# Splitting the weights of every sublayer by transfers of GpSimd's queue

## The chip, the cores and the metric

The kernel runs on one core of a Trainium2 chip. A core has five engines that run side by side, each through its own queue of instructions in order: TensorE (PE; the loading of its weights is shown as PEld), VectorE (DVE), ScalarE (ACT), GpSimd (POOL) and SyncE (SP), which here only issues transfers. Sixteen DMA engines move data between memory and the on-chip buffers. The metric is the device time of one execution in microseconds (us), lower is better.

## The reference, cut to what matters

Two blocks follow each other on x of 512 tokens x 1024 features, in float32. The first has two layers of three sublayers: a feed forward, a mixer (stick-breaking attention in layer 0, a gated linear recurrence in layer 1) and a second feed forward, each behind a norm and a modulation by shift, scale and gate that come from a vector c. The second block has two hybrid layers with three attentions and gates. All heavy work is products of activations with float32 weights:

```python
def swiglu(h, w_gu, w_down):
    g, u = jnp.split(h @ w_gu, 2, axis=-1)
    return (jax.nn.silu(g) * u) @ w_down
...
        h, g = sublayer_input(x, norm_g[layer, 0], mod[:, 0])
        x = x + MACARON_W * g * swiglu(h, ffn_w_gu[layer, 0], ffn_w_down[layer, 0])
```

## The kernel before

Activations are kept transposed, features on the 128 partitions and the 512 tokens along the row. TensorE takes a rounded format (float32r) at its full rate, so that each float32 operand is split in two rounded parts, high and low, and every product is made of three matmuls: high by high, high weight by low activation, low weight by high activation (`proj`, lines 571 to 585; `proj_tok`, 587 to 601, has the weights as the moving side).

All weights come from one array `ws` of blocks of 128 x 1024 that the host has put in the order of use. The order is a list of entries (`layout`, line 197): a weight entry ("w") holds eight slots of 128 x 128; an entry "mod" holds a block of the modulation matrix. There are 493 weight entries and 144 modulation blocks. The eight segments are named ffn00, sb, ffn01, ffn10, lru, ffn11, hy0 and hy1. In ffn00 56 and in ffn10 48 modulation blocks stand between the weights, in ffn01 24, and 16 at the very start.

`stream_dma` (line 451) issues the loads ahead on SP's queue, of 512 KB each, into a ring of four tiles `raw` (`RAW = 4`, line 319), shared by both kinds of entry. `stream_step` (line 476) takes the next entry. A modulation block is multiplied with c and summed by DVE (line 485). A weight entry is split in two chunks of 512 columns, each in three steps: ACT copies the chunk, rounding it, to `wh` (line 497; in one stretch of the recurrence, where `act_busy` is set at line 1319, DVE does it at line 495), and POOL or DVE subtracts the copy from the raw weights into `wl` (line 503). Which of the two is chosen by a credit (`pool_low`, lines 498 to 502): POOL in the mixers, in the hybrid layers and at the start of a sublayer, DVE in the rest of the feed forwards. `wh` and `wl` have five buffers each (`AHEAD + 1`). After the split of the second chunk the raw tile is free (line 513).

```python
    def ahead(self, c):
        while self.w_conv < c + 1 + self.look and self.e_conv < len(self.entries):
            self.stream_step()
```

`take` (line 558) hands TensorE's code the high and low part of the next slots and calls `ahead`, so that the split is written into the program four chunks ahead of the use. At the start of each sublayer of the first block the shift part of the modulation is not known in time; there the products are made without it and a correction is summed by DVE from the plain raw weights (`shifts`, line 518; `first_slots`, line 177, lists these slots).

The order of instructions on an engine comes from two sources. The mixers' steps are generators that `pump` starts when a count of TensorE's time (`vt`) has passed their `yield`; within `with self.tc.manual_schedule()` (in `begin`, line 870, and at the kernel's start) the written order holds, and elsewhere a scheduler orders each engine's queue by the priority of the written order and its own model of times. Waits between engines, and for a free buffer of a tile's ring, are put in by the framework.

Other work that the steps of the prediction touch: POOL's selection in the stick-breaking attention (line 1132), its squares of the residual (lines 635 and 639), its sums of gates (line 1816); DVE's split of rotated queries and keys (line 1375); ACT's square roots and gates in the recurrence (lines 1277 and 1284); SP's copies of queries and keys into stacked tiles (line 981) and the loads and stores of x (lines 833 and 1880).

Of the kernel before, what the change touches and what calls it, by code (L numbers as in the profile page):

```python
# [22 lines left out]
F32 = mybir.dt.float32  # L23
F32R = mybir.dt.float32r
I32 = mybir.dt.int32
AF = mybir.ActivationFunctionType
OP = mybir.AluOpType
# [149 lines left out]
def first_slots(segs):  # L177

    out = {}
    slot = 0  # L180
    for name, jobs, _ in segs:
        for job in jobs:
            for kt in rows_of(job):
                for j, (_, _, cols) in enumerate(job[1]):
                    if name in LATE and job[0] == "first":
                        out[slot] = (LATE[name], kt, j)
                    elif name == "ffn00" and job[0] in ("gu6", "gu7"):
                        out[slot] = ((0, 0), kt, int(job[0][2:]))
                    slot += len(cols) // 128
    return out  # L190


def rows_of(job):
    return range(job[2]) if isinstance(job[2], int) else job[2]
# [120 lines left out]
class Kern:  # L315
# [117 lines left out]
    def stream_init(self, entries):  # L433
        self.entries = entries
        self.e_dma = 0
        self.e_conv = 0
        self.raws = {}
        self.parts = {}
        self.slot = 0
        self.w_conv = 0  # L440
        self.n_w, self.kept = 0, []
        self.in_ring = 0
        self.full = set()
        self.wshift = {}
        self.inv = None
        self.look = self.AHEAD
        self.act_busy = False
        self.pool_low = 0.0
        self.pool_credit = 0.0

    def stream_dma(self):
        nc = self.nc
        while self.e_dma < len(self.entries):
            src = self.io["ws"][self.e_dma]
            e = self.entries[self.e_dma]
            if e[0] == "w" and self.n_w < self.KEEP:
                raw = [self.t("keep"), self.t("keep")]
                self.n_w += 1
                for j in range(2):
                    nc.sync.dma_start(raw[j], src[:, 512 * j:512 * j + 512])  # L460
            elif self.in_ring < self.RAW:
                raw = self.wpool.tile([128, 1024], F32, name=self.name("raw"), tag="raw", bufs=self.RAW)
                nc.sync.dma_start(raw, src)
                self.in_ring += 1
                if e[:2] == ("mod", (0, 0, 1)):
                    x = self.t("x")
                    nc.sync.dma_start(x, self.io["xT"][e[2]])
                    if e[2] == 4:
                        nc.sync.dma_start(self.ident, self.io["k_ident"])
                    self.x.append(x)  # L470
            else:
                break
            self.raws[self.e_dma] = raw
            self.e_dma += 1

    def stream_step(self):
        self.stream_dma()
        e = self.entries[self.e_conv]
        raw = self.raws[self.e_conv]
        nc = self.nc  # L480
        if e[0] == "mod":
            vec, m = e[1], e[2]
            if vec not in self.mods:
                self.mods[vec] = self.modp.tile([128, 8], F32, name=self.name("mod"), tag="mod", bufs=12)
            nc.vector.tensor_tensor_reduce(raw, raw, self.cact, 1.0, 0.0, OP.mult, OP.add, accum_out=self.mods[vec][:, m:m + 1])  # L485
            self.full.add((vec, m))
            if m == KD - 1 and vec != (0, 0, 1):
                self.mod_end(vec, 0, KD)
        else:
            j = self.w_conv % 2  # L490
            w = raw[j] if type(raw) is list else raw[:, 512 * j:512 * j + 512]
            h = self.wpool.tile([128, 512], F32R, name=self.name("wh"), tag="wh", bufs=self.AHEAD + 1)
            l = self.wpool.tile([128, 512], F32R, name=self.name("wl"), tag="wl", bufs=self.AHEAD + 1)
            if self.act_busy:
                nc.vector.tensor_copy(h, w)
            else:
                nc.scalar.copy(h, w)  # L497
            self.pool_credit += self.pool_low
            eng = nc.vector
            if self.pool_credit >= 1.0:  # L500
                self.pool_credit -= 1.0
                eng = nc.gpsimd
            eng.tensor_tensor(l, w, h.bitcast(F32), OP.subtract)  # L503
            self.parts[self.w_conv] = (h, l)
            if type(raw) is list:
                self.kept.append((4 * self.w_conv, w))
            else:
                self.shifts(w, 4 * self.w_conv)
            self.w_conv += 1
            if j == 0:  # L510
                return
        if type(raw) is not list:
            self.in_ring -= 1
        del self.raws[self.e_conv]
        self.e_conv += 1
        self.stream_dma()
# [41 lines left out]
    def take(self, n):  # L558
        c, o = divmod(self.slot, 4)
        self.ahead(c)  # L560
        self.parts.pop(c - 1, None)
        self.slot += n
        h, l = self.parts[c]
        return h[:, 128 * o:128 * (o + n)], l[:, 128 * o:128 * (o + n)]
# [1334 lines left out]
    def body(self):  # L1899
        nc = self.nc  # L1900
        segs = segments()
        self.stream_init(layout(segs))
        self.segs = {n: list(j) for n, j, _ in segs}
        self.late = first_slots(segs)
        self.mods = {}
        self.twice = False
        self.quick = False
        self.sq = {}
        self.gain, self.save, self.hnext, self.xd = None, False, [], []
        self.vecs = self.const.tile([128, NVEC], F32, name="vecs")  # L1910
        self.ident = self.const.tile([128, 128], F32, name="ident")
        self.ones = self.const.tile([128, 128], F32, name="ones")
        self.cact = self.const.tile([128, 1024], F32, name="cact")

        def shown(name):
            if self.upto == name:
                for m in range(KD):
                    nc.sync.dma_start(self.io["out"][m], self.x[m])
                return True

        for l in range(2):
            for i in range(2):
                self.jobs = self.segs[f"ffn{l}{i}"]
                if (l, i) == (1, 1):
                    self.twice = self.save = True
                    self.fgain = self.modp.tile([128, 8], F32, name="gain")
                    nc.vector.tensor_tensor(self.fgain, self.vec("final_norm_g"), self.vec("norm_g_2", 0, 8), OP.mult)
                self.ffn(l, i)
                if shown(f"ffn{l}{i}"):
                    return  # L1930
                if i:
                    continue
                if l == 0:
                    self.jobs = self.segs["sb"]
                    self.stick()
                else:
                    with self.tc.manual_schedule():
                        self.lru_consts()
                    self.jobs = self.segs["lru"]
                    self.lru()  # L1940
                if shown("sb" if l == 0 else "lru"):
                    return
        self.hybrid_consts()
        for l in range(2):
            self.jobs = self.segs[f"hy{l}"]
            self.hybrid(l)
            if shown(f"hy{l}"):
                return
        self.last_norm()
# [28 lines left out]
```

## Time and profile before

| | us |
|---|---|
| median of 3 runs | 3132.27 |
| lowest and highest | 3131.87, 3133.31 |
| the profiled execution, its own time | 3133.14 |
| its span, first to last instruction | 3131.3 |
| TensorE busy in the span | 3007.2 |
| DVE, ACT, POOL busy | 1921.7, 1321.7, 1072.8 |

The span is what the trace sees of an execution; 1.84 us lie around it. A row of a group gives the line, engine and operation, the tiles written and read, the shapes, the count, then busy time, the mean of one in ns, and the engine's idle time just before with what ended it. Instructions that only issue a transfer or wait are not counted as busy. "DMA share" is the mean busy share of the sixteen DMA engines.

### The profile page before, as it was taken

The numbers are of one execution on the slowest core, as the hardware profiler recorded it, in microseconds if no ns is written. First come the engines' busy times: TensorE is split into PE (matmuls) and PEld (weight loads), VectorE is DVE, ScalarE is ACT, GpSimd is POOL, SyncE is SP. The second block draws the span as 40 slices with busy tenths as digits, with TensorE's granted clock in tenths as the row PEclk, the third lists the DMA queues.
The fourth block names the chain that finished last, engine by engine and source line by source line (L and its number), as shares of the span: only waits on it lengthen the run. The fifth ranks groups of instructions, "written<-read, shape, count | busy, mean of one in ns | idle before, by whom it ended". The sixth has DMA issues, their size and how long they took to land. (4 is left out here: it accounts for less than half of the span.)

```text
span 3131.3 us, 39192 instructions
## 1 busy us (share of the span) xinstructions
PE 3007.2 (96%) x13752; PEld 2474.4 (79%) x13752; DVE 1921.7 (61%) x3455; ACT 1321.7 (42%) x2520; POOL 1072.8 (34%) x828
## 2 busy tenths in 40 slices
PE   7999999989999999999899999999999999999998
PEld 5788877778888888887788888888787778878776
DVE  7844467685445654569773334587766547877643
ACT  3332245543332333226543333355455434655552
POOL 4455744440001100025430002433334674333356
PEclk9999999999999999999999999999999999999999
DMA  6454545324343344542222223543441336324322
GB/s 243 163 195 172 209 120 142 102 68 147 130 140 128 135 162 149 181 175 74 88 88 101 94 105 111 136 135 105 120 132 62 108 124 177 103 88 128 102 78 91
DMA packets 132358, 400.03 MB, mean 128 GB/s; under 512 B 18496, under 2 KB 19008, under 8 KB 132160
## 3 DMA queue, kind: packets, MB, share of 16 engines
q1 hardware_dynamic: 132160, 397.51, 39.1%
q8 instruction: 109, 1.79, 0.2%
q14 instruction: 89, 0.73, 0.1%
HBM read 342.91 MB, written 6.30 MB: 112 GB/s over the span
## 5 line engine op out<-in xcount | busy, mean ns | idle before, releaser
L503 POOL TENSOR_TENSOR wl<-raw,wh 128x512 fp32r<-128x512 f32 x576 | 803.0, 1402 | 940.9 <-ACT wh L497 897.2
L497 ACT CAST wh<-raw 128x512 fp32r<-128x512 f32 x968 | 596.4, 620 | 1152.7 <-PE mm L417 993.0
L417 PE MATMUL mm<-hH,wh 128*128 128x512 f32 x1584 | 620.9, 392 | 12.4 <-ACT ge L1284 9.8
L417 PE MATMUL mm<-hL,wh 128*128 128x512 f32 x1584 | 620.3, 392 | 4.1 <-DVE hL L722 3.4
L417 PE MATMUL mm<-hH,wl 128*128 128x512 f32 x1584 | 619.4, 391 | 0.3 <-POOL wl L503 0.3
L503 DVE TENSOR_TENSOR wl<-raw,wh 128x512 fp32r<-128x512 f32 x394 | 290.0, 737 | 363.0 <-ACT wh L497 360.6
L417 PE MATMUL mm<-gH,wh 128*128 128x512 f32 x1016 | 409.7, 403 | 1.9 <-ACT wh L497 1.8
L417 PE MATMUL mm<-gH,wl 128*128 128x512 f32 x1016 | 401.9, 396 | 1.3 <-POOL wl L503 1.3
L417 PE MATMUL mm<-gL,wh 128*128 128x512 f32 x1016 | 401.6, 395 | 0.0
L417 PEld LDWEIGHTS mm<-hH,wh 128*128 128x128 f32 x1584 | 299.1, 189 | 76.0 <-ACT ge L1284 10.2
L417 PEld LDWEIGHTS mm<-hL,wh 128*128 128x128 f32 x1584 | 299.0, 189 | 68.5 <-DVE hL L722 5.5
L417 PEld LDWEIGHTS mm<-hH,wl 128*128 128x128 f32 x1584 | 298.9, 189 | 62.3 <-POOL wl L503 0.7
L485 DVE CUSTOM_DVE_ANT_0 raw<-raw,cact 128x1024 f32<-128x1024 f32 x144 | 209.2, 1456 | 177.4 <-DMA raw<-ws 167.0
L417 PE MATMUL mm<-aH,wh 128*128 128x512 f32 x704 | 273.9, 389 | 0.0
L417 PE MATMUL mm<-aH,wl 128*128 128x512 f32 x704 | 273.9, 389 | 0.0
L635 POOL TENSOR_TENSOR sq<-x 128x512 f32<-128x512 f32 x7 | 8.1, 1151 | 736.9 <-DVE x L970 710.0
L417 PEld LDWEIGHTS mm<-gH,wl 128*128 128x128 f32 x1016 | 192.4, 189 | 42.1 <-POOL wl L503 2.6
L417 PEld LDWEIGHTS mm<-gH,wh 128*128 128x128 f32 x1016 | 193.4, 190 | 36.2 <-ACT wh L497 2.3
L417 PEld LDWEIGHTS mm<-gL,wh 128*128 128x128 f32 x1016 | 193.3, 190 | 32.9
L1029 DVE TENSOR_TENSOR wide<-T,wide 128x128 fp32r<-128x128 f32 (+3 forms) x192 | 94.2, 511 | 102.5 <-ACT wide L1026 93.8
L417 PEld LDWEIGHTS mm<-aH,wh 128*128 128x128 f32 x704 | 132.1, 188 | 27.6
L417 PEld LDWEIGHTS mm<-aH,wl 128*128 128x128 f32 x704 | 132.1, 188 | 27.4
(302 smaller groups left out, 4825.0 us busy)
## 6 DMA issues: line engine op xcount, KB each, us to landing
raw<-ws SPq DMA_DIRECT2D x629, 512.0 KB, 3.3
ks<-rH SPq DMA_DIRECT2D x80, 128.0 KB, 3.1
kl<-rL SPq DMA_DIRECT2D x80, 128.0 KB, 2.4
qs<-rH SPq DMA_DIRECT2D x56, 128.0 KB, 3.9
qs<-rL SPq DMA_DIRECT2D x56, 128.0 KB, 3.9
keep<-ws SPq DMA_DIRECT2D x16, 256.0 KB, 5.7
ks<-qkH SPq DMA_DIRECT2D x32, 128.0 KB, 2.8
kl<-qkL SPq DMA_DIRECT2D x32, 128.0 KB, 2.4
```

What stands on the lines that cost most here:

```text
L417: self.nc.tensor.matmul(out, lhsT, rhs, start=start, stop=stop, skip_group_check=True)
L485: nc.vector.tensor_tensor_reduce(raw, raw, self.cact, 1.0, 0.0, OP.mult, OP.add, accum_out=self.mods[vec][:, m:m + 1])
L497: nc.scalar.copy(h, w)
L503: eng.tensor_tensor(l, w, h.bitcast(F32), OP.subtract)
L635: nc.gpsimd.tensor_tensor(q, self.x[m], self.x[m], OP.mult)
L1029: nc.vector.tensor_tensor(dst(pt[1], o, n, step), src(c, n, step), dst(pt[0], o, n, step).bitcast(F32), OP.subtract)
```

## The change

A weight entry without any slot that needs the plain weights (and not among the first eight) is loaded from POOL's queue into the raw tile with its type given as float32r, which rounds it: the tile is then the high part itself, and no `wh` is made. For each chunk ACT writes the negated high part to `wl`, and a second transfer from POOL's queue adds the plain weights from memory to it, which leaves the low part. The raw tile counts as used until TensorE's code has gone past its second chunk (`held`); the release is looked at in `take`. By the layout 464 of the 493 weight entries take this way: 58 in ffn00, 28 in sb, 62 in each of ffn01, ffn10 and ffn11, 28 in lru, 82 in each of hy0 and hy1.

```diff
--- before.py
+++ after.py
@@ -187,6 +187,25 @@
                     elif name == "ffn00" and job[0] in ("gu6", "gu7"):
                         out[slot] = ((0, 0), kt, int(job[0][2:]))
                     slot += len(cols) // 128
+    return out
+
+
+def inlined(segs, entries, names, late):
+
+    out = set()
+    ends = []
+    n = 0
+    for name, jobs, _ in segs:
+        n += sum(len(cols) // 128 for job in jobs for _ in rows_of(job) for _, _, cols in job[1])
+        ends.append((n, name))
+    slot = 0
+    for i, e in enumerate(entries):
+        if e[0] != "w":
+            continue
+        name = next((name for end, name in ends if slot < end), None)
+        if name in names and not any(slot + j in late for j in range(8)):
+            out.add(i)
+        slot += 8
     return out
 
 
@@ -444,6 +463,7 @@
         self.wshift = {}
         self.inv = None
         self.look = self.AHEAD
+        self.held = []
         self.act_busy = False
         self.pool_low = 0.0
         self.pool_credit = 0.0
@@ -458,6 +478,11 @@
                 self.n_w += 1
                 for j in range(2):
                     nc.sync.dma_start(raw[j], src[:, 512 * j:512 * j + 512])
+            elif e[0] == "w" and self.in_ring < self.RAW and self.inline(self.e_dma):
+                raw = self.wpool.tile([128, 1024], F32, name=self.name("raw"), tag="raw", bufs=self.RAW)
+                nc.gpsimd.dma_start(raw.bitcast(F32R), src)
+                raw = (raw, src)
+                self.in_ring += 1
             elif self.in_ring < self.RAW:
                 raw = self.wpool.tile([128, 1024], F32, name=self.name("raw"), tag="raw", bufs=self.RAW)
                 nc.sync.dma_start(raw, src)
@@ -473,6 +498,12 @@
             self.raws[self.e_dma] = raw
             self.e_dma += 1
 
+
+    INLINE = "ffn00", "sb", "ffn01", "ffn10", "lru", "ffn11", "hy0", "hy1"
+
+    def inline(self, e):
+        return e in self.inlined
+
     def stream_step(self):
         self.stream_dma()
         e = self.entries[self.e_conv]
@@ -488,6 +519,21 @@
                 self.mod_end(vec, 0, KD)
         else:
             j = self.w_conv % 2
+            if type(raw) is tuple:
+
+                h = raw[0].bitcast(F32R)[:, 512 * j:512 * j + 512]
+                l = self.wpool.tile([128, 512], F32R, name=self.name("wl"), tag="wl", bufs=self.AHEAD + 1)
+                nc.scalar.mul(l, h.bitcast(F32), -1.0)
+                nc.gpsimd.dma_start(l, raw[1][:, 512 * j:512 * j + 512], accum_op=OP.add)
+                self.parts[self.w_conv] = (h, l)
+                self.w_conv += 1
+                if j == 0:
+                    return
+                self.held.append(self.w_conv)
+                del self.raws[self.e_conv]
+                self.e_conv += 1
+                self.stream_dma()
+                return
             w = raw[j] if type(raw) is list else raw[:, 512 * j:512 * j + 512]
             h = self.wpool.tile([128, 512], F32R, name=self.name("wh"), tag="wh", bufs=self.AHEAD + 1)
             l = self.wpool.tile([128, 512], F32R, name=self.name("wl"), tag="wl", bufs=self.AHEAD + 1)
@@ -559,6 +605,10 @@
         c, o = divmod(self.slot, 4)
         self.ahead(c)
         self.parts.pop(c - 1, None)
+        while self.held and self.held[0] <= c:
+            self.held.pop(0)
+            self.in_ring -= 1
+        self.stream_dma()
         self.slot += n
         h, l = self.parts[c]
         return h[:, 128 * o:128 * (o + n)], l[:, 128 * o:128 * (o + n)]
@@ -1902,6 +1952,7 @@
         self.stream_init(layout(segs))
         self.segs = {n: list(j) for n, j, _ in segs}
         self.late = first_slots(segs)
+        self.inlined = inlined(segs, self.entries, self.INLINE, self.late)
         self.mods = {}
         self.twice = False
         self.quick = False
```

## Rows read from the trace of the kernel before

**Rows 1.** The page, span and part 1: busy us, share of the span, instructions.
```profile
span 3131.3 us, 39192 instructions
...
PE 3007.2 (96%) x13752; PEld 2474.4 (79%) x13752; DVE 1921.7 (61%) x3455; ACT 1321.7 (42%) x2520; POOL 1072.8 (34%) x828
```

**Rows 2.** Stages ffn00 to hy1: length, busy us (count) by engine, clock, DMA, GB/s.
```profile
core 0: us, PE busy (x) PEld busy (x) DVE busy (x) ACT busy (x) POOL busy (x), PEclk, DMA share, GB/s
0.00:402.00 402.00, 374.75 (x1615) 305.95 (x1616) 238.40 (x335) 131.75 (x221) 222.85 (x154) 0.98 0.56 194
402.00:670.00 268.00, 250.61 (x1210) 204.77 (x1209) 189.43 (x308) 143.61 (x285) 118.48 (x128) 0.97 0.40 111
670.00:1041.00 371.00, 364.46 (x1610) 301.88 (x1609) 199.10 (x296) 123.80 (x204) 35.59 (x24) 0.99 0.37 128
1041.00:1405.00 364.00, 362.89 (x1612) 300.17 (x1611) 214.56 (x335) 118.51 (x196) 30.66 (x21) 1.00 0.47 165
1405.00:1610.00 205.00, 187.78 (x807) 152.66 (x806) 162.41 (x193) 111.54 (x176) 98.25 (x68) 0.96 0.24 84
1610.00:1972.00 362.00, 361.73 (x1608) 299.58 (x1607) 155.34 (x224) 123.70 (x203) 39.72 (x28) 1.00 0.29 102
1972.00:2548.00 576.00, 552.44 (x2653) 454.28 (x2652) 386.93 (x889) 289.10 (x627) 265.86 (x203) 0.99 0.39 115
2548.00:3131.00 583.00, 552.58 (x2650) 455.09 (x2648) 375.47 (x878) 279.68 (x613) 261.34 (x205) 0.98 0.36 110
```

**Rows 3.** TensorE's waits, whole span: us in total, times, longest us.
```profile
PE z L417 <- DVE mx L1399: 7.7, 9, 2.3
...
PE mm L417 <- ACT wh L497: 1.8, 1, 1.8
...
PE mm L417 <- POOL wl L503: 1.6, 3, 0.7
```

**Rows 4.** The page, part 5: busy us, mean ns | idle before, its releaser.
```profile
L503 POOL TENSOR_TENSOR wl<-raw,wh 128x512 fp32r<-128x512 f32 x576 | 803.0, 1402 | 940.9 <-ACT wh L497 897.2
L497 ACT CAST wh<-raw 128x512 fp32r<-128x512 f32 x968 | 596.4, 620 | 1152.7 <-PE mm L417 993.0
...
L485 DVE CUSTOM_DVE_ANT_0 raw<-raw,cact 128x1024 f32<-128x1024 f32 x144 | 209.2, 1456 | 177.4 <-DMA raw<-ws 167.0
```

**Rows 5.** Groups of instructions, DVE, in hy0.
```profile
L1375 DVE TENSOR_TENSOR rL<-r,rH 128x512 fp32r<-128x512 f32 x24 | 26.6, 1110 | 10.8 <-ACT rH L1373 10.6
```

**Rows 6.** Groups of instructions, DVE, from 1700 to 1800 us, in ffn11.
```profile
L503 DVE TENSOR_TENSOR wl<-raw,wh 128x512 fp32r<-128x512 f32 x37 | 25.6, 691 | 46.6 <-ACT wh L497 46.6
```

**Rows 7.** TensorE's waits in lru.
```profile
PE mm L417 <- ACT ge L1284: 9.8, 1, 9.8
PE z L417 <- DVE xL L1252: 4.2, 1, 4.2
```

**Rows 8.** Groups of instructions, POOL, in sb.
```profile
L1132 POOL TENSOR_SCALAR_AFFINE_SELECT beta<-beta 128x128 f32<-128x128 f32 x64 | 31.5, 512 | 50.0 <-ACT beta L1126 42.7 <-PE mm L417 7.1
```

**Rows 9.** Windows at full DMA load, in ffn00, in ffn10; as rows 2.
```profile
10.00:25.00 15.00, 13.09 (x46) 10.27 (x47) 11.26 (x23) 7.08 (x13) 5.06 (x4) 1.00 1.04 397
110.00:400.00 290.00, 287.62 (x1263) 238.13 (x1264) 144.48 (x187) 89.07 (x153) 171.60 (x118) 0.99 0.56 192
1041.00:1389.00 348.00, 346.89 (x1541) 286.94 (x1540) 203.89 (x321) 114.48 (x189) 28.01 (x19) 1.00 0.48 169
```

**Rows 10.** DMA issues: size, median us from issue to landing.
```profile
raw<-ws SPq DMA_DIRECT2D x629, 512.0 KB, 3.3
...
xd<-x SPq DMA_DIRECT2D x16, 256.0 KB, 3.0
x<-xd SPq DMA_DIRECT2D x16, 256.0 KB, 5.2
```

**Rows 11.** Timeline in lru: start us, us, engine, line.
```profile
1502.43 1.85 DVE L495 CAST wh<-raw 128x512 fp32r<-128x512 f32 x2
...
1513.68 2.70 ACT L497 CAST wh<-raw 128x512 fp32r<-128x512 f32 x5
```

## The prediction

> **What bounds the kernel now.** I read the page's busy times first: TensorE is busy for 3007.2 of 3131.3 us, GpSimd (POOL) for 1072.8 [rows 1]. A share of 96% over the whole span hides where the rest lies, so the second view is the table by stage [rows 2]. The four feed forward stages are full: the last of them has 361.73 busy us in 362. Its 1608 matmuls in 362 us give 0.225 us each, so an entry (eight 128x128 blocks, three products each, 24 matmuls) lasts 5.40 us and a half, a chunk of 512 columns, 2.70 us. No change to the splitting of weights can make such a stage shorter. TensorE idles in the mixers: 17.4 us in sb (268 minus 250.6), 17.2 in lru, 23.6 in hy0, 30.4 in hy1 (its last part is the closing norm, which no weight enters), and 27 us in ffn00, most of it start-up. The third view is what TensorE waits for: a weight's high half for 1.8 us, a low half for 1.6 us, against 7.7 us for one maximum of a softmax alone [rows 3]. So the splitting is not late now, and what it can give back is only what it takes from VectorE (DVE), ScalarE (ACT) and POOL while they work for the mixers. Its size: 803.0 us on POOL and 596.4 us on ACT [rows 4], and a DVE share in the feed forward stages.
>
> **The sum** is made against the profiled execution, 3133.14 us (span 3131.3 and 1.84 around it); the median of the three timed runs, 3132.27, lies 0.87 lower.
>
> **Part 1, what goes away.** By the layout 464 of the 493 weight entries are taken by the new path; 29 (the ones whose shift sums need the plain weights, and the first eight) stay. For 928 chunks the high half needs no ACT copy and the low half no subtraction. ACT gains nothing: the negation that replaces the copy has the same shape, and I price it with the copy's 620 ns [rows 4]. POOL loses some 550 subtractions of 1402 ns, DVE some 380 of its own. In the feed forward stages this is off the path, behind a full TensorE: 0 us. In the mixers it matters through DVE. There a DVE subtraction with two operands in SBUF takes 1110 ns while POOL is busy 266 of 576 us [rows 2, 5], and the same form takes 691 ns in a stretch where POOL does nothing [rows 6]: 0.4 us lost for each such instruction. With 24 of that line in hy0 alone, and lines beside it of the same kind, some 30 us of DVE work go per hybrid. TensorE sees only the part that stood at the end of a wait. I take 12 of the 54 us that the hybrids idle, 3 of sb's 17.4, and 8 of the 14.0 us that lru waits on a chain through DVE and ACT [rows 7]: **-23 us**. Ends: 0 (those waits are latency elsewhere) and -45 (half of all idle time in the mixers).
>
> **Part 2, the transfers.** Each entry now has three transfers from POOL's queue: 512 KB rounded into the tile, and two of 256 KB that add to a negated copy. None of these is in the trace. Their **issue** on POOL I bound by POOL's shortest frequent instruction, 0.51 us [rows 8], and by its subtraction, 1.40 us [rows 4]; I take 1.0. Three are 3.0 us of POOL per 5.40 us entry (1.5 to 4.2), so POOL does not become the bound unless an issue costs 1.8 us.
>
> Their **transfer time**: at full load the 16 DMA engines moved 397 GB/s [rows 9]. The 0.524 MB of an entry each 5.40 us are 97 GB/s, a share of 0.25. An accumulation reads its source again, and its destination in SBUF too, so it costs between one and three times a plain load of the same bytes, or a share of 0.25 to 0.75; I take 0.37, one and a half, nearer the load row because SBUF is read beside HBM. On top of the shares of now [rows 2, 9]: 0.93 in ffn00's long stretch (0.56 now), 0.85 in ffn10 (0.48), 0.74 in ffn01, 0.66 in ffn11. Nothing is full: 0 us.
>
> The Trainium skill says otherwise: "Collectives: The Full Stack" (The bandwidth ceiling: the fold count and why AG ≠ RS ≠ AR) has the add itself free and its two source reads halve the rate. By that rule the share is 0.50, ffn00's stretch comes to 1.06, 290 x 0.06 = 17 us are added, and the sum is 3134; no row here shows it.
>
> Their **lateness**: before, a raw tile was free again once split, four chunks ahead of its use. Now it is the high half itself and is held until TensorE has used it, so the four raw tiles are the whole prefetch. Where only weights stream, a load starts when TensorE leaves an entry and its sum is needed three entries later, 16.2 us. The chain is issue 1.0, landing 4.0, ACT 0.62, issue 1.0, landing 4.0: 10.6 us. The landings lie between 3.0 us (a 256 KB store; the raw load has 3.3) and 5.2 us (a 256 KB load) [rows 10], so the chain lies between 7.9 and 13.8 us: always in time, 0 us. In ffn00 and ffn10 a modulation block stands beside nearly every entry, 104 in all, and holds one of the four tiles for its own load and its 1.46 us on DVE [rows 4], about 5 us. That leaves 11.2 us, and 10.6 just fits: 0 us; the upper end would cost (13.8 - 11.2)/3 = 0.87 us an entry, 90 us.
>
> **Part 3, waits and queues.** On POOL a load now waits for TensorE to leave a tile and an accumulation for ACT's negation; behind them stand sb's selections, the squares of the residual and the gate sums. POOL's subtraction waited for ACT in the same way (897.2 us, [rows 4]) with the same work behind it: 0 us. SP's queue loses 464 loads and its waits for raw tiles; the copies of keys and queries are no longer behind them: at most a few tenths each, 0 us. The five stage starts and the kernel's own start keep their written order, with loads on POOL ahead of low halves that are still subtracted there: **+3 us** (0 to 10). In lru the old path gave two chunks to DVE while ACT was held by its square roots; the new path always uses ACT. Those two negations would come after 1513.68, when ACT resumes copies [rows 11], and their sums some 5 us later, while four chunks ahead of 1502.43, when DVE began them, cover 10.8 us, to 1513.2: **+4 us** (0 to 8).
>
> **Sum:** 3133.1 - 23 + 3 + 4 = **3117 us**.
>
> **Rivals.** *B, the mixed stretches fall behind* (slower). Place: ffn00 and ffn10, where modulation blocks and weights share four tiles. It decides once the chain is over 11.2 us or an accumulation costs over 1.75 times its load (0.44 of share is free at 0.56). For it: the middle case has 0.6 us to spare, transfers slow each other there, and POOL issues in order, so one late load delays the next. Against it: raw loads land in 3.3 us at today's 0.56. With a chain of 13 us: (13 - 11.2)/3 x 104 = 62 us, so 3117 + 62 = about 3180 us (3139 to 3225).
> *C, the transfers bound all feed forward layers* (slower). At three times a load the shares are 1.31, 1.12, 1.22 and 1.04, so 290 x 0.31 + 371 x 0.12 + 364 x 0.22 + 362 x 0.04 = 229 us: 3346 us. An issue of over 1.8 us on POOL does the same. It decides from 2.8 times on. For it: nothing in the trace shows an add done by a transfer. [...]
> *D, hidden anyway.* The mixers' waits are latency, DVE's relief shows nowhere, and small losses cancel the rest; or an accumulation costs twice a load and ffn00's long stretch alone takes 17 us back (share 1.06): 3132 to 3134 us, within 0.2%. The second of these is what the page on collectives gives, and I count a third of D's chance to it.
>
> A page by which neither B nor C would happen is the Trainium skill's "DMA: Bandwidth & Descriptors" (Anatomy of one DMA — SWDGE (gpsimd) path): about 2.0 us and bytes at 436 GB/s, an estimate of 3.2 us for 512 KB and 2.6 for 256 KB. The raw load's 3.3 us, issued by SP, agrees; no run here shows one from POOL.
>
> **How the numbers follow.** A measurement of this kernel can tell 0.2%, 6.3 us, from no change: faster is under 3126, slower over 3138.5. My forecast has 0.41 and its own range is 3098 to 3126; D has 0.15, B 0.25, C 0.19. So faster 0.41, same 0.15, slower 0.44: two slow mechanisms together weigh a little more than the one gain, but each alone less. The range runs from 3098 to 3250: it takes in forecast, D and B, and leaves out most of C.
>
> **What would show it.** Right: DVE's subtraction in the hybrids near 700 ns instead of 1110, POOL's subtractions reduced to some 60, TensorE still at 99% or more in ffn01 and ffn11, stage lengths of the mixers down by 2 to 4%. Wrong by B: TensorE waiting for wl in ffn00 and ffn10 alone, and those two stages longer. Wrong by C: ffn11 longer than 362 us, with a DMA share near 1 or POOL busy throughout. D: DVE faster and the mixers no shorter.

## The result, and the profile after

The changed kernel takes **3504.65 us** (median of four runs, 3481.96 to 3512.92) against 3132.79 for the kernel before on the same chip: a ratio of 1.117, 95% interval 1.1142 to 1.1199. The prediction of 3117 us had the wrong sign, and its range ended at 3250. The profiled execution has a span of 3511.2 us, 379.9 more than before; the sums below are made against it.

The page of the changed kernel (span, part 1, groups of part 5, the queues of part 3, issues of part 6) answers to [rows 1, 4, 10]:

```profile
span 3511.2 us, 39455 instructions
...
PE 3134.3 (89%) x13752; PEld 2530.6 (72%) x13752; DVE 1538.1 (44%) x3074; ACT 1309.5 (37%) x2524; POOL 1358.1 (39%) x1671
...
q0 software_dynamic: 200448, 486.63, 66.0%
q1 hardware_dynamic: 65344, 154.21, 14.5%
...
L527 POOL DMA_DIRECT2D wl<-ws x928 | 819.9, 971 | 1540.6 <-ACT wl L526 1503.1
L526 ACT ACTIVATE wl<-raw 128x512 fp32r<-128x512 f32 x928 | 567.3, 628 | 1618.3 <-DMA raw<-ws 709.4
...
L483 POOL DMA_DIRECT2D raw<-ws x464 | 332.3, 744 | 436.4 <-PE mm L436 326.9
...
raw<-ws POOLq DMA_DIRECT2D x464, 512.0 KB, 6.1
wl<-ws POOLq DMA_DIRECT2D x928, 256.0 KB, 5.4
...
kl<-rL SPq DMA_DIRECT2D x80, 128.0 KB, 6.9
```

L483 is the rounding load, L526 the negation, L527 the transfer that adds. TensorE has 127 us more of busy time for the same 13752 matmuls, and its mean granted clock is 0.954 where it was 0.986, so part of the loss is a lower clock; the rest is idling. Where, the stages tell (columns as in [rows 2]):

```profile
0.00:563.00 563.00, 425.35 (x1617) 329.91 (x1618) 208.33 (x335) 128.71 (x222) 184.76 (x213) 0.90 0.75 192
563.00:833.00 270.00, 249.56 (x1210) 202.95 (x1209) 170.94 (x310) 144.39 (x285) 103.38 (x155) 0.97 0.74 164
833.00:1259.00 426.00, 384.06 (x1610) 306.52 (x1609) 119.82 (x176) 116.56 (x203) 169.70 (x207) 0.96 0.81 188
1259.00:1758.00 499.00, 410.70 (x1609) 320.72 (x1608) 140.13 (x217) 112.55 (x195) 165.76 (x204) 0.91 0.77 186
1758.00:1960.00 202.00, 187.33 (x807) 151.52 (x806) 124.46 (x174) 115.86 (x179) 97.42 (x112) 0.97 0.74 157
1960.00:2325.00 365.00, 363.69 (x1610) 301.10 (x1609) 76.32 (x103) 124.26 (x204) 175.03 (x216) 1.00 0.91 190
2325.00:2912.00 587.00, 556.91 (x2652) 458.91 (x2651) 358.72 (x889) 287.25 (x625) 232.60 (x286) 0.98 0.85 186
2912.00:3511.00 599.00, 556.68 (x2649) 458.98 (x2647) 339.37 (x878) 279.95 (x614) 229.41 (x284) 0.97 0.84 181
```

Against [rows 2] ffn00 has 161 us more, ffn10 135, ffn01 55: 351 of the 380. These three are the feed forward layers that have modulation blocks between their weights. ffn11, which has none, has 3 more, at full clock and with the DMA engines at 0.91. The mixers have +2 (sb), -3 (lru), +11 and +16 (hybrids). What TensorE waits for, over the whole span, in place of [rows 3]:

```profile
PE mm L436 <- DMA wl<-ws: 260.0, 123, 6.5
...
PE z L436 <- DMA kl<-rL: 5.5, 4, 1.8
```

A low half that has not landed costs 260.0 us, where the old one cost 1.6; a copy of keys (`kl`) is now waited for as well. To see why it is late, the timeline of POOL, and then of ACT, in ffn00 (start us, us, engine, line):

```profile
314.17 1.76 POOL L527 DMA_DIRECT2D wl<-ws  x2 [9.66 <-ACT wl L526]
315.25 1.25 POOL L483 DMA_DIRECT2D raw<-ws  x1
324.01 1.73 POOL L527 DMA_DIRECT2D wl<-ws  x2 [7.51 <-ACT wl L526]
325.09 1.21 POOL L483 DMA_DIRECT2D raw<-ws  x1
```
```profile
313.25 1.16 ACT L526 ACTIVATE wl<-raw 128x512 fp32r<-128x512 f32 x2 [8.76 <-DMA raw<-ws]
...
322.80 1.15 ACT L526 ACTIVATE wl<-raw 128x512 fp32r<-128x512 f32 x2 [7.62 <-DMA raw<-ws]
```

The load that starts at 315.25 lands by 322.80, ACT negates it, POOL starts its two accumulations at 324.01, and only then, at 325.09, does the next load start: one entry in 9.84 us, where TensorE uses one in 5.40. The round is made of the load's landing (from its issue until the data is there; 7.55 us), the negation (1.21) and the issue of the two accumulations (1.08); the landing of the accumulations is not in it. Load, negation and accumulation, which should overlap over several entries, follow each other in one **loop on POOL's queue**. In ffn11 the same instructions stand otherwise:

```profile
2104.69 0.55 POOL L483 DMA_DIRECT2D raw<-ws  x1 [1.28 <-PE mm L436]
2105.28 0.85 POOL L527 DMA_DIRECT2D wl<-ws  x1
...
2109.83 0.55 POOL L483 DMA_DIRECT2D raw<-ws  x1 [0.95 <-PE mm L436]
```

Here a load waits for TensorE to leave a tile, 5.14 us after the load before. The view of line 483's instructions gives the counts, from 110 to 540 us in ffn00 and then from 2000 to 2300 us in ffn11:

```profile
L483 POOL DMA_DIRECT2D raw<-ws x49: 543/1225/1958, 122.6 to 532.3; - x49
...
  PE mm L436: 5.0, 4
  DVE mod L516: 2.5, 1
```
```profile
L483 POOL DMA_DIRECT2D raw<-ws x55: 550/554/1167, 2001.0 to 2295.1; - x55
...
  PE mm L436: 48.9, 50
```

In ffn11 50 of 55 loads waited for TensorE; in ffn00 44 of 49 waited for nothing but their place behind other work in POOL's queue. By the first and last start in these rows a load goes out every 8.5 us on the mean in ffn00, so 9.84 us is a round longer than the mean.

### The profile page after: what moved, and what is told of

The parts are those of the page before. It is cut to its first block, busy times and chain, and to the rows that moved or that the text cites. A ratio compares the mean times of both kernels' runs of the same rounds, so it can differ in the third digit from the quotient of the medians.

```text
span 3511.2 us, 39455 instructions
## 1 busy us (share of the span) xinstructions
PE 3134.3 (89%) x13752; PEld 2530.6 (72%) x13752; DVE 1538.1 (44%) x3074; ACT 1309.5 (37%) x2524; POOL 1358.1 (39%) x1671
## 5 line engine op out<-in xcount | busy, mean ns | idle before, releaser
L527 POOL DMA_DIRECT2D wl<-ws x928 | 819.9, 971 | 1540.6 <-ACT wl L526 1503.1
L526 ACT ACTIVATE wl<-raw 128x512 fp32r<-128x512 f32 x928 | 567.3, 628 | 1618.3 <-DMA raw<-ws 709.4
L436 PE MATMUL mm<-hH,raw 128*128 128x512 f32 x1580 | 635.0, 402 | 6.4 <-DVE xc L1293 3.7
L436 PE MATMUL mm<-hL,raw 128*128 128x512 f32 x1580 | 633.1, 401 | 0.5 <-DVE hL L772 0.4
L483 POOL DMA_DIRECT2D raw<-ws x464 | 332.3, 744 | 436.4 <-PE mm L436 326.9
L436 PE MATMUL mm<-gH,raw 128*128 128x512 f32 x896 | 362.7, 405 | 0.0
L436 PEld LDWEIGHTS mm<-hH,raw 128*128 128x128 f32 x1580 | 308.6, 195 | 69.9 <-DVE xc L1293 4.1
L436 PEld LDWEIGHTS mm<-hL,raw 128*128 128x128 f32 x1580 | 307.3, 195 | 67.3 <-DVE hL L772 1.7
L436 PE MATMUL mm<-gL,raw 128*128 128x512 f32 x896 | 354.3, 395 | 0.0
L436 PE MATMUL mm<-aH,raw 128*128 128x512 f32 x704 | 291.7, 414 | 2.6 <-DMA raw<-ws 2.6
```

The source lines that it names most:

```text
L436: self.nc.tensor.matmul(out, lhsT, rhs, start=start, stop=stop, skip_group_check=True)
L483: nc.gpsimd.dma_start(raw.bitcast(F32R), src)
L526: nc.scalar.mul(l, h.bitcast(F32), -1.0)
L527: nc.gpsimd.dma_start(l, raw[1][:, 512 * j:512 * j + 512], accum_op=OP.add)
```

## The experiments

Two theories stood against each other. **L**, the loop: with a modulation block in the ring there are too few tiles for weights, so that each load stands directly behind the previous entry's accumulations on POOL's queue. **W**, the work of the transfers: an addition costs the DMA engines so much that the stretches with modulation blocks can't go faster, however they are queued. All ratios are to the kernel before on the same chip.

**More tiles: raw5 and raw6.** The ring gets five or six tiles. The space comes from `wh`, which few entries still use, and in raw6 from two slots of another buffer. This is raw6; raw5 keeps 74 slots and has `RAW = 5`.

```diff
-    NSLOT = 74
-    RAW = 4
+    NSLOT = 72
+    RAW = 6
...
-            h = self.wpool.tile([128, 512], F32R, name=self.name("wh"), tag="wh", bufs=self.AHEAD + 1)
+            h = self.wpool.tile([128, 512], F32R, name=self.name("wh"), tag="wh", bufs=3)
```

> Five raw tiles in place of four (the high-half ring cut to three to make room), nothing else. Theory L (loop): in the stretches with modulation blocks POOL's queue has each load right behind the accumulations of the entry before, so load, landing, negation and accumulation of one entry follow each other without overlap, 9.4 us an entry; a fifth tile puts the load one entry ahead and the loop goes: about 3165 us, ffn00 near 400 and ffn10 near 372. Rival W (transfer work): rounding and adding cost the DMA engines so much that those stretches are full; more tiles change nothing: over 3450 us.

> Six raw tiles (high-half ring three, 72 in place of 74 general tiles). Theory L: what is left of lateness goes too, 3150 to 3165 us, no wait for wl over 1 us in ffn00 or ffn10. Rival W: over 3450 us, DMA share unchanged. Whether anything below 3132 us is left decides if the mixers gain at all: the changed kernel's mixers are 28 us longer than before, so neither theory expects it.

Measured: raw5 3287.86 us, ratio 1.0495 (1.047 to 1.0521); raw6 3283.81 us, 1.0473 (1.045 to 1.0496). Windows of raw6 in ffn00, ffn10 and ffn11:

```profile
110.00:440.00 330.00, 282.40 (x1192) 228.18 (x1192) 99.09 (x166) 84.84 (x147) 125.91 (x157) 0.95 0.93 241
1120.00:1520.00 400.00, 360.80 (x1532) 292.04 (x1531) 120.55 (x196) 114.31 (x192) 164.00 (x202) 0.96 0.91 225
1760.00:2090.00 330.00, 330.00 (x1457) 273.27 (x1456) 59.68 (x69) 113.59 (x184) 160.44 (x201) 1.00 0.97 198
```

One tile gives back 217 us, the second 4 more, which is within the noise. L is right about the first. The second is no help, and W is one reason: in raw6 the stretch in ffn00 has the DMA engines at 0.93 (0.56 before, [rows 9]) and still lasts longer. Neither theory alone gives 3284, and there is a third effect. Under L no wait for `wl` over 1 us was to be left; here is what TensorE waited for in raw6's ffn00 (0 to 456 us), and POOL and DVE at its longest wait, which began at 343.5:

```profile
PE mm L436 <- DMA wl<-ws: 51.2, 16, 12.6
```
```profile
343.90 1.03 POOL L685 TENSOR_TENSOR sqt<-x 128x512 f32<-128x512 f32 x1 [12.35 <-DVE x L1020]
```
```profile
341.92 1.23 DVE L516 CUSTOM_DVE_ANT_0 raw<-raw,cact 128x1024 f32<-128x1024 f32 x1 [3.24 <-DMA raw<-ws]
```

POOL stood 12.35 us at a square of the residual (line 685), with loads and accumulations behind it in its queue. The square waited for DVE's new x (line 1020), and that stood behind modulation sums (line 516) that waited for their blocks. ACT stood 13.80 us for the same x. From 110 to 440 us POOL waited 52.4 us for x at such squares, with four tiles 5.1 us (110 to 540). So late modulation blocks can hold up the weights through the queues of DVE and ACT as well; how much of raw6's loss this is, no run takes apart.

**Modulation blocks in a tile of their own: modtile.** Past the first two vectors a modulation block gets the one tile `rawm`, and the four tiles of the ring are for weights alone.

```diff
-            elif self.in_ring < self.RAW:
+            elif e[0] == "mod" and e[1][:2] != (0, 0) and self.mod_ring < 1:
+                raw = self.wpool.tile([128, 1024], F32, name=self.name("rawm"), tag="rawm", bufs=1)
+                nc.sync.dma_start(raw, src)
+                self.mod_ring += 1
+            elif self.in_ring < self.RAW and (e[0] == "w" or e[1][:2] == (0, 0)):
```

> Modulation blocks after the first two vectors get one tile of their own; the weights keep four tiles to themselves. Theory L with the blocks as the cause of the short ring: like five tiles, about 3165 us, though the single block tile may make DVE's sums late (they are due far ahead, 0 us). If four tiles alone are too few whatever shares them: about 3500 us. Rival W: over 3450 us.

Measured: 3402.87 us, 1.0862 (1.0844 to 1.088). The same five tiles as raw5, but 115 us slower: a shared ring is the better use of them. Loads are issued in the order of use, so a single tile for modulation blocks probably holds up the weights behind them; that was not measured by itself, and the run does not decide between L and W.

**The loop in a stage that has no modulation blocks: ffn11_3.** The new path is used in ffn11 alone, with three tiles; a tile is given back a little earlier in the order written, which by itself makes loads earlier.

```diff
-    RAW = 4
+    RAW = 3
...
-    INLINE = "ffn00", "sb", "ffn01", "ffn10", "lru", "ffn11", "hy0", "hy1"
+    INLINE = ("ffn11",)
...
-        self.ahead(c)
-        self.parts.pop(c - 1, None)
         while self.held and self.held[0] <= c:
             self.held.pop(0)
             self.in_ring -= 1
         self.stream_dma()
+        self.ahead(c)
+        self.parts.pop(c - 1, None)
```

> The new path in ffn11 alone, where no modulation block stands, with three raw tiles (a tile given back just before the next chunk is written, so that three suffice). In POOL's queue 47 of its 62 loads then stand right behind the accumulations of the entry before. Theory L: ffn11 is 3 us longer in each of them, 362 to about 500 us, in all near 3270. Rival W: an entry asks 4.2 of 5.4 us of the DMA engines, nothing is full: ffn11 stays at 365, in all near 3135.

Measured: 3260.78 us, 1.0414 (1.0393 to 1.0435). The window of ffn11, TensorE's waits in it, and POOL's timeline:

```profile
1607.00:2098.00 491.00, 408.47 (x1608) 318.86 (x1607) 78.18 (x103) 117.02 (x203) 177.22 (x211) 0.93 0.62 140
```
```profile
PE mm L436 <- DMA wl<-ws: 82.2, 45, 5.9
```
```profile
1806.82 1.75 POOL L527 DMA_DIRECT2D wl<-ws  x2 [5.67 <-ACT wl L526]
1807.95 1.19 POOL L483 DMA_DIRECT2D raw<-ws  x1
1815.58 1.78 POOL L527 DMA_DIRECT2D wl<-ws  x2 [6.44 <-ACT wl L526]
1816.81 1.66 POOL L483 DMA_DIRECT2D raw<-ws  x2
```

ffn11 goes from 362 us to 491, with the pattern of ffn00: each load directly behind two accumulations, 8.86 us apart. The DMA engines are busy 0.62 of it, so that full DMA engines, W's reason, have no part here. With four tiles the same stage took 365. This shows that the number of tiles alone makes or breaks the loop. It also bounds the clock's share. The engine idled up to 5.9 us at a time, 82.2 us in all, and the granted clock, 1.00 in the stage before [rows 2], was 0.93 on the mean, going between its two levels. The 1608 matmuls have 408.47 busy us against 361.73, 47 more of the 129. At most 0.07 x 491 = 34 of these are the clock, an estimate; the rest stays open (the profile models where a matmul ends).

**Only where no modulation block stands: plain.** The new path stays in sb, lru, ffn11 and the hybrids.

```diff
-    INLINE = "ffn00", "sb", "ffn01", "ffn10", "lru", "ffn11", "hy0", "hy1"
+    INLINE = "sb", "lru", "ffn11", "hy0", "hy1"
```

> The new path only in sb, lru, ffn11, hy0 and hy1, so in no stretch with modulation blocks. Theories L and W both put the loss in ffn00, ffn01 and ffn10, so those go back to 391, 371 and 364 us; what is left are the mixers and ffn11, 28 us longer than before in the changed kernel: about 3160 us. If the mixers gain once SP's queue and the DMA engines are calmer: below 3126 us.

Measured: 3166.25 us, 1.0105 (1.009 to 1.012). The three stages return to 405, 370 and 363 us, 350 us less than in the changed kernel, which places that part of the loss in the new path there, whichever way it works; what remains lies mostly in the hybrids (585 and 603 us, 9 and 20 more than before).

**Transfers that write instead of adding: no_add and no_add6.** The second transfer of each chunk has the same bytes and the same place, but leaves out the addition, once with four and once with six tiles (as raw6).

```diff
-                nc.gpsimd.dma_start(l, raw[1][:, 512 * j:512 * j + 512], accum_op=OP.add)
+                nc.gpsimd.dma_start(l, raw[1][:, 512 * j:512 * j + 512])
```

> The second transfer of each chunk writes the rounded weights over the negated copy and adds nothing (so the low halves are wrong, the work on all engines is the same); four raw tiles as in the changed kernel. If a 2 KB row then costs 84 ns in place of 178, an entry with a modulation block asks 4.0 us of the DMA engines in place of 5.5. Theory L (loop): the load still stands behind the accumulations, only its landing shortens, some 2.4 us lost in each of 106 entries: 3350 to 3400 us. Rival W (transfer work): the mixed stretches have room again, about 3165 us.

> The same without the adding, with six raw tiles. If the 150 us that six tiles left are the adding's cost to the DMA engines (share 0.93 there): ffn00 near 395 and ffn10 near 366, in all 3140 to 3165 us. If they are lateness of another kind: about 3280 us.

Measured: no_add 3236.33 us, 1.0336 (1.0315 to 1.0357); no_add6 3150.06 us, 1.006 (1.004 to 1.0081). No_add lies between L (the loop stays, a little shorter) and W (the addition was the cost): each holds a part. The loop is still there: from 110 to 440 us in ffn00, 39 of 47 loads waited for nothing but their place. But a load lands in 5.5 us where it took 7.5 in the changed kernel:

```profile
raw<-ws POOLq DMA_DIRECT2D x47, 512.0 KB, 5.5
```

The weights' queue in the kernel before and in no_add (span 3237.3), from their pages:

```profile
q1 hardware_dynamic: 132160, 397.51, 39.1%
```
```profile
q0 software_dynamic: 200448, 486.63, 51.8%
```

From these comes **the price of adding**. In time of all 16 engines, q0 took 0.660 x 3511.2 = 2317 us in the changed kernel and 0.518 x 3237.3 = 1677 in no_add. The 243.3 MB that left SP's queue had cost 0.391 x 3131.3 - 0.145 x 3511.2 = 715 us. If no_add's two halves cost alike, 838 each, adding 243.3 MB costs 2317 - 838 = 1479 us, 2.07 times the plain loads of before. The trace's records of single packets bear the split out: in the changed kernel the packets of 2 KB that add sum to 1486 us and those of 4 KB that round to 799, in no_add to 859 and 782. The Trainium skill's rule in "Collectives: The Full Stack" (The bandwidth ceiling: the fold count and why AG ≠ RS ≠ AR), stated there for a reduction between cores, that the second source read halves the rate, agrees with that factor of about two. Three stages of no_add6 (ffn00, ffn10, hy0), whose boundaries are 0, 1056 and 2004 us:

```profile
0.00:422.00 422.00, 380.71 (x1619) 307.52 (x1620) 197.00 (x336) 131.24 (x220) 140.72 (x214) 0.97 0.80 259
1056.00:1442.00 386.00, 370.46 (x1609) 303.56 (x1608) 130.37 (x215) 116.84 (x195) 121.86 (x205) 0.98 0.76 238
2004.00:2570.00 566.00, 548.87 (x2652) 454.40 (x2651) 353.68 (x888) 290.66 (x626) 178.00 (x287) 0.99 0.73 193
```

With six tiles the addition is worth 134 us (raw6 to no_add6). With four it is worth 268, and six tiles are worth 221 with it and 86 without. The two causes are not a sum: slow transfers make each round of the loop longer, and few tiles make it a loop. What is left in no_add6 is 20 us more in ffn00 and 22 in ffn10, and 3, 5, 10 and 3 less in sb, lru and the two hybrids. TensorE's longest waits for `wl` in the two, 7.4 and 6.4 us, stand again beside a POOL that waited 11.8 and 11.5 us at a square for DVE's x.

**In the recurrence alone: lru_only.**

```diff
-    INLINE = "ffn00", "sb", "ffn01", "ffn10", "lru", "ffn11", "hy0", "hy1"
+    INLINE = ("lru",)
```

> The new path in the recurrence alone, the one stage that was shorter in the changed kernel (201.8 against 204.8 us). If that holds by itself: 3129 us. If it was the disturbed neighbourhood: 3132 us.

Measured: 3132.15 us (ten runs) against 3131.53, 1.0003 (0.9993 to 1.0012): no gain. The one stage that the full change had shortened gives nothing by itself, and none of the versions run here beats the kernel before. Loading on another queue than POOL's was not tried.

## Why the prediction was wrong, step by step

**Part 2, lateness: the step that failed.** It had the chain at 10.6 us against a budget of 11.2, "just fits: 0 us". Both its sizes and its form were off. Size: issued from POOL between 110 and 540 us, the landings are, by the issues of that stretch,

```profile
wl<-ws POOLq DMA_DIRECT2D x100, 256.0 KB, 5.7
raw<-ws POOLq DMA_DIRECT2D x49, 512.0 KB, 7.5
```

where 4.0 each was taken from rows between 3.0 and 5.2 of SP's queue [rows 10]. The two landings alone are 13.2 us. Form: being late was priced at a third of the excess per entry, as if three entries were always in work together. But POOL issues in order, and a load behind accumulations waits for the landing and the negation that these wait for. The excess of the round, without the accumulations' landing, is then paid by each entry in full: 9.84 - 5.40 = 4.4 us in the timeline above, where the upper end had 0.87. On the mean a load went out every 8.5 us there and every 7.7 in ffn10 (1263.6 to 1692.2 us, 57 loads): 49 x 3.1 = 152 and 57 x 2.3 = 131 us, of the 161 and 135 that the two stages lost. The order was in the program: a load is written when a tile is given back, and with the ring short of tiles that comes after the accumulations of the entry before. The prediction named this ("POOL issues in order") only as an argument for B.

**Rival B** had the place (ffn00 and ffn10, TensorE waiting for `wl`) and its first condition came true (13.2 us of landings against 11.2 for the whole chain); so did the second, an accumulation at 2.07 against 1.75. Its price of 62 us was 234 short of the 296 that these two stages lost, mostly since it used the same third, and ffn01's 55 us with its 24 blocks were not in it. The range rested on that price, and so it missed.

**Part 2, transfer time.** 1.5 times a load was taken, 2.07 measured: inside the bounds, but on the other side of B's point. That SBUF is read beside HBM, the reason for 1.5, is shown by no run. The rounding load was counted at the price of a plain one; at 838 against 715 us it is 1.17 times that, if the halves are alike. The plain load was underpriced as well: 0.25 goes by 397 GB/s, but 715 us for 464 entries are 1.54 us each, a share of 0.29 of 5.40. The new transfers took 2317 / 464 = 4.99 us an entry, a share of 0.92, not 0.62. On the shares of before ffn00's stretch would want 0.56 - 0.29 + 0.92 = 1.19 of the engines and ffn10's 1.11; 290 x 0.19 + 348 x 0.11 = 93 us, an estimate from these rows, that no order of queues could save. raw6 has 54 us more than before in ffn00 and 52 in ffn10, together 106, but 42 of these are there without the addition too (no_add6), so the two can't be set against each other as they stand. The 17 us by the Trainium skill's rule in "Collectives: The Full Stack" (same section as above) were nearer than the sum, and still small beside the loop.

**Issue.** 1.0 us taken; 0.55 for a load and 0.85 for an accumulation where POOL is otherwise quiet, 744 and 971 ns on the mean. Three make 2.25 us in ffn11's 5.40: right, POOL is not the bound.

**Rival C** is refuted as it was put: ffn11 stays at 365 us with the DMA engines at 0.91.

**Rival D**: its first half, relief that shows nowhere, is what the mixers have, and lru_only as a kernel.

**Part 1, -23 us in the mixers.** The relief is there, but not its yield. In hy0 the subtraction of [rows 5] went from 1110 to 814 ns, not to 691:

```profile
L1425 DVE TENSOR_TENSOR rL<-r,rH 128x512 fp32r<-128x512 f32 x24 | 19.5, 814 | 31.3 <-ACT rH L1423 31.3
```

TensorE's waits in hy0, first for the changed kernel, then for no_add6:

```profile
PE mm L436 <- DMA wl<-ws: 7.4, 5, 2.8
...
PE z L436 <- DMA kl<-rL: 2.7, 2, 1.5
```
```profile
PE z L436 <- DMA qs<-rL: 4.3, 3, 2.1
...
PE mm L436 <- DMA wl<-ws: 1.1, 1, 1.1
PE z L436 <- DMA kl<-rL: 1.0, 1, 1.0
```

Summing all rows of that view, TensorE waited in hy0 22.6 us before, 0.5 of it for transfers, and 29.2 after, 10.6 of it for transfers. So 3.5 us of waits for engines went and 10.1 of waits for transfers came. In no_add6 it is 16.1, 6.4 of it for transfers, and its mixers are 21 us shorter than before: near the 23 predicted. So the term's size came out where the second transfers do not add and six tiles are there, though with a subtraction at 815 ns and not 691. Part 3 had costed the copies of keys and queries at a few tenths, for their place in SP's queue; that they share the DMA engines with the weights' transfers, and land in 6.9 us instead of 2.4 (`kl`), was not in the sum. In no_add6 they take 6.0, so the additions are the smaller part of this.

**Part 3.** The +4 us in lru are not seen (202 and 205 us in the changed kernel and in lru_only, 205 before). The +3 of the stage starts can't be told from the rest. The squares of the residual, at 0 us, did cost time once the ring was longer (raw6).

## What to carry to other kernels

Before a step is moved to an in-order queue, write down one round of that queue with the number of buffers that the stretch really leaves: where a load stands behind work that waits for the load before it, the chain up to that work's issue is paid for each item, and one buffer more can be worth more than any faster instruction. Price a transfer that adds at about two plain ones in DMA time, and look at who else uses those engines, small copies on a critical path above all. A step that "just fits" needs a rival with the price of not fitting worked out from the order of the queue.

## What was not expected of the hardware

- An adding transfer of 256 KB took 0.85 us of POOL to issue where a rounding load of 512 KB took 0.55, and the means rose to 971 and 744 ns in the whole kernel. Without the addition the same 256 KB took 0.53 to 0.56 us (no_add, 300 to 330 us).
- The landing of a transfer from POOL's queue is not a constant: the 512 KB load took 7.5 us behind two accumulations in ffn00 and 5.6 in ffn11; over the whole kernel it took 6.1, and 4.2 in no_add. The Trainium skill's "DMA: Bandwidth & Descriptors" (Anatomy of one DMA — SWDGE (gpsimd) path), which by the estimate in the prediction gives 3.2 us, is below all of them.
- TensorE stayed full, at clock 1.00, beside DMA engines that were busy 0.97 of the time (raw6, 1760 to 2090 us): a share near 1 alone is no proof of a bound.
